# Two attention layers in one run each: queries and keys made a head ahead, projections 200 columns ahead, fewer small operations

## The chip, the cores and the metric

The kernel runs on one core of a Trainium2 chip. The metric is the device time of one execution in microseconds (us): 1171.78 us median of three runs (1171.17 to 1171.89). The engines are TensorE (PE, with its weight loads PEld), VectorE (DVE), ScalarE (ACT), GpSimd (POOL) and SyncE (SP), which issues most DMAs here. Each engine works off its own instructions in the order in which they stand.

## The reference

A decoder trunk of two layers on 512 tokens of 1024 features, all in float32. Each layer is attention and then a squared-ReLU MLP, both behind an RMS norm and with a residual.

```python
for layer in range(DEPTH):
    h = rms_norm(x, g_mix[layer])
    x = x + (even_mixer if layer % 2 == 0 else odd_mixer)(h, ...)
    h = rms_norm(x, g_mlp[layer])
    x = x + squared_relu_mlp(h, w_up[layer], w_down[layer])
```

Both mixers project h with one weight matrix, normalize q and k per head of 64 features (RMS, with a gain), attend and project the heads' outputs back. Layer 0 has eight heads of kind a (a mixture of dilated windows with a distance penalty) and eight of kind b (a window of 128, with two heads of k and v and a sink per head). Layer 1 has 16 heads of kind c (causal, with a bias c[t] - c[s] from a cumulated forget gate).

## The kernel before, in words

Every float32 matmul is three: the operands are split into a high part and the rest, and the products high x high, rest x high and high x rest are added up. For a weight tile the split is `parts` (a cast on ACT or POOL makes `whi`, a subtraction on DVE or POOL, L155, makes `wlo`).

In attention two streams of work are interleaved. The dense stream is `project` (L231 to L233): groups of 256 or 512 columns of q and k, or of v, over 32 pairs of feature chunk and token tile, and at the end of a layer `out_part`, the output projection. The results stand in four PSUM banks (`pA`); `norm_heads` copies them out (ACT), sums squares (ACT, then L250 on DVE), takes the reciprocal square root in small operations on DVE, and multiplies (L260), two token tiles on DVE and two on POOL. `prep_v` does the same for v without the norm.

The other stream is `attend`. It goes through pairs of heads. `get` makes a pair's q and k: `head_T` transposes (`qkT`, L267) into a bank of the other four (`pB`), and `prep_q` and `prep_k` write for each head a tile with the high part in one half of the partitions and the rest in the other (q), or both parts in both halves (k; the second half is copied by a DMA, L290). Each of the four query tiles i of a head is then scored (`S`, L325, L326), reduced with its bias on DVE (L339, which gives p and the negative maximum), exponentiated on ACT (L342, which gives the denominator), and scaled by the denominator's reciprocal (L345, then L350 on POOL or, for the last tile, L347 on ACT). In `values`, transposes (`PT`, L362) and products with v (`O`, L382) follow; a head's values are made within the scores of the next head.

`run` decides how the streams are woven. It takes a piece of the dense stream whenever that is behind its share, where `lead` shifts the share, and it is called once for each section: in layer 0 for a heads 0 to 3, for the b heads, and for the last a heads; in layer 1 once for each group of four heads. A section ends when its dense stream does; what is left of the attention is then run off. So a group's q and k are first asked for in the section after the one that projects them.

A scheduler then orders the instructions of each engine from this program order and from estimates of their durations, and gives out buffers as they come free.

Of the kernel before, what the change touches and what calls it, by code (L numbers as in the profile page):

```python
# [37 lines left out]
NORM = 'vgvg'  # L38
PSC = 'ggga'
GRAIN = 4  # L40
STARTPIN = 4
# [8 lines left out]
AHEAD = ()  # L50
# [13 lines left out]
LEADS = (0.0, 0.0, -0.16, 0.33, -0.3, -0.23, -0.09)  # L64
LAGS = (1, 1, 1)
NB = 86
# [6 lines left out]
def trunk(ctx, tc, x, g_mix, g_mlp, w_in_even, a_q_gain, a_k_gain, b_q_gain, b_k_gain, b_sinks,  # L73
# [118 lines left out]
    def layer_attention(li, hT, w_in, w_out, stats=None):  # L192


        with ExitStack() as c2:
# [44 lines left out]
            def norm_heads(outs, nh, sq_tag="sq", sq_bufs=1 + li):  # L240
# [11 lines left out]
                for t in range(NT):  # L252
                    nc.vector.tensor_scalar(v[:, t, :nh], ss[:, t, :nh], 1.0 / HD, ecol[:, t:t + 1],
                                            op0=OP.mult, op1=OP.add)
                rs = small.tile([P, NT, 8], F32, tag="rs", name="rs")
                rsqrt_small(rs[:, :, :nh], v[:, :, :nh])
                for t in range(NT):
                    q = qk[t // 2][:, t % 2, :w].rearrange("p (h d) -> p h d", d=HD)
                    eng = nc.gpsimd if NORM[t] == "g" else nc.vector
                    eng.tensor_mul(q, q, rs[:, t, :nh].unsqueeze(2).to_broadcast([P, nh, HD]))  # L260
# [9 lines left out]
            def prep_q(qk, off):  # L270

                pt = head_T(qk, off)
                q = ap.tile([P, 2, 512], F32R, tag="Q", bufs=2, name="Q")
                for h in range(2):
                    r = slice(h * HD, (h + 1) * HD)
                    r2 = slice((1 - h) * HD, (2 - h) * HD)
                    nc.scalar.copy(q[r, h], pt[r])
                    nc.vector.tensor_sub(q[r2, h], pt[r], q[r, h].bitcast(F32))
                return q

            def prep_k(qk, off, g):

                pt = head_T(qk, off)
                ks = []
                for h in range(2):
                    k = ap.tile([P, 2, 512], F32R, tag="K", bufs=3, name="K")
                    r = slice(h * HD, (h + 1) * HD)
                    r2 = slice((1 - h) * HD, (2 - h) * HD)
                    scale_split(k[r, 0], k[r, 1], pt[r], g[r])
                    nc.sync.dma_start(k[r2].bitcast(F32), k[r].bitcast(F32))  # L290
# [11 lines left out]
            def scores(q, k, j, kind, h, pr):  # L302
# [11 lines left out]
                rden = small.tile([P, NT], F32, tag="rden", name="rden")  # L314
                for i in range(NT):
# [29 lines left out]
                    nc.vector.reciprocal(rden[:, i:i + 1], den[:, i:i + 1])  # L345
                    if PSC[i] == "a":
                        nc.scalar.activation(p[:, :nv], p[:, :nv], AF.Copy, scale=rden[:, i:i + 1])  # L347
                    else:
                        eng = nc.gpsimd if PSC[i] == "g" else nc.vector
                        eng.tensor_scalar(p[:, :nv], p[:, :nv], rden[:, i:i + 1], 1.0, op0=OP.mult, op1=OP.mult)  # L350
# [52 lines left out]
            def attend(get, koff, V, vslot, kind, h0, np_, y0):  # L403

                for p_ in range(np_):
                    q, kk = get(p_)
# [23 lines left out]
            def run(att, n_att, dense, n_dense, lead=0.0):  # L430
# [12 lines left out]
                if att is not None:  # L443
                    for _ in att:
                        pass
# [798 lines left out]
```

## Time and profile before

| | |
|---|---|
| median of three runs | 1171.78 us |
| profiled execution | 1169.99 us, of which 1168.2 us span |
| PE busy | 1146.4 us (98%), 6256 matmuls |
| DVE busy | 879.8 us (75%), 1870 instructions |
| ACT busy | 646.6 us (55%) |
| POOL busy | 203.0 us (17%) |
| granted TensorE clock | 1.0 throughout |

Attention of layer 0 takes the time up to 228 us, its MLP the time to about 580 us, attention of layer 1 that to 831 us, and the second MLP the rest. In a busy row stand the time, the share of the span and the count of instructions. A group's row gives line, engine, operation, output and inputs with shapes, count, busy time, mean ns of one, and idle time of the engine just before with what ended it. A wait's row gives who waited for whom, total us, times, and the longest. Since matmuls are pipelined, a matmul's row is longer than the time to the next matmul's start.

### The profile page before, as it was taken

The page shows a single profiled execution, that of the slowest core. Times are in us where ns is not written, and L with a number is a line of the kernel's source. Part 1 is how long each engine was busy: PE and PEld are TensorE (multiplying, and loading weights), DVE is VectorE, ACT ScalarE, POOL GpSimd, SP SyncE. Part 2 cuts the span into 40 slices and gives each one's busy share as a digit, 9 for nine tenths or more (in the row PEclk, how much of TensorE's full clock was granted, in tenths as well). Part 3 has the DMA queues.
Part 4 walks back from the last instruction along what each step waited for, and adds up shares of the span by engine and source line. Part 5 has one row for each costly group of instructions (what it writes and reads, how often), then busy time and mean ns, then how long its engine had stood idle before and what let it go on. Part 6 is the DMA issues. An engine that isn't in the chain of part 4 may idle for free.

```text
span 1168.2 us, 17496 instructions
## 1 busy us (share of the span) xinstructions
PE 1146.4 (98%) x6256; PEld 981.4 (84%) x6256; DVE 879.8 (75%) x1870; ACT 646.6 (55%) x1349; POOL 203.0 (17%) x296
## 2 busy tenths in 40 slices
PE   8999989999999999999999999999999999999998
PEld 7987878887988988988887888888888888888887
DVE  7878999969947847855647877788858749669676
ACT  6556867655445545444335685656756455465452
POOL 1445434200000000000155445332100000000000
PEclk9999999999999999999999999999999999999999
DMA  7532024132332332333443323343430721623403
GB/s 257 160 91 73 19 73 145 58 123 73 101 117 91 91 108 91 96 121 108 148 127 109 103 89 110 100 124 112 163 106 3 232 91 51 202 73 108 148 34 109
DMA packets 100655, 126.57 MB, mean 108 GB/s; under 512 B 6184, under 2 KB 79944, under 8 KB 100568
## 3 DMA queue, kind: packets, MB, share of 16 engines
q1 hardware_dynamic: 99384, 121.23, 34.0%
q10 hardware_dynamic: 608, 2.13, 0.5%
q0 software_dynamic: 576, 2.10, 0.4%
q8 instruction: 49, 0.80, 0.3%
q14 instruction: 38, 0.31, 0.1%
HBM read 112.29 MB, written 6.32 MB: 102 GB/s over the span
## 4 chain that ended last, share of the span: by engine, by line
PE 82%; DVE 9%; DMA 3%; ACT 2%; POOL 1%; issue 1%; SPq 0%; ACTq 0%; POOLq 0%; DVEq 0%
PE up L164 10%; PE up L167 10%; PE up L168 10%; PE pj L231 4%; PE pj L233 4%; PE pj L232 4%; PE O L382 3%; PE PT L362 2%; PE Y L1023 2%; PE Y L1022 2%; PE Y L1020 2%; PE op L168 2%; PE op L164 2%; PE op L167 2%; PE S L325 2%; DVE wlo L155 1%
## 5 line engine op out<-in xcount | busy, mean ns | idle before, releaser
L164 PE MATMUL up<-xin,whi 128*128 128x512 f32 x512 | 200.5, 392 | 0.0
L168 PE MATMUL up<-xin,whi 128*128 128x512 f32 x512 | 199.3, 389 | 0.0
L167 PE MATMUL up<-xin,wlo 128*128 128x512 f32 x512 | 199.2, 389 | 0.0
L769 ACT CAST whi<-wraw 128x512 fp32r<-128x512 f32 x228 | 139.2, 619 | 105.5 <-PE up L168 47.3
L770 DVE TENSOR_TENSOR wlo<-wraw,whi 128x512 fp32r<-128x512 f32 x228 | 151.7, 686 | 53.7 <-ACT whi L769 53.5
L168 PEld LDWEIGHTS up<-xin,whi 128*128 128x128 f32 x512 | 96.1, 188 | 20.1
L164 PEld LDWEIGHTS up<-xin,whi 128*128 128x128 f32 x512 | 96.1, 188 | 19.9 <-issue 0.2
L167 PEld LDWEIGHTS up<-xin,wlo 128*128 128x128 f32 x512 | 96.2, 188 | 19.7 <-issue 0.2
L342 ACT ACTIVATE P<-P,negm 128x128 f32<-128x128 f32 (+5 forms) x128 | 69.6, 544 | 51.8 <-DVE negm L339 47.9
L231 PE MATMUL pj<-whi,hn 128*128 128x512 f32 (+2 forms) x256 | 88.7, 346 | 0.0
L951 ACT ACTIVATE u<-up 128x512 f32<-128x512 f32 x64 | 38.3, 598 | 90.9 <-PE up L168 90.9
L233 PE MATMUL pj<-whi,hn 128*128 128x512 f32 (+2 forms) x256 | 86.9, 339 | 0.0
L232 PE MATMUL pj<-wlo,hn 128*128 128x512 f32 (+2 forms) x256 | 86.8, 339 | 0.0
L152 POOL TENSOR_SCALAR whi<-wraw 128x512 fp32r<-128x512 f32 x88 | 61.1, 696 | 141.5 <-PE pj L233 121.3
L790 DVE TENSOR_TENSOR t<-u 128x256 f32<-128x256 f32 x56 | 23.2, 424 | 63.3 <-ACT u L1094 61.5
L155 POOL TENSOR_TENSOR wlo<-wraw,whi 128x512 fp32r<-128x512 f32 x48 | 64.4, 1345 | 20.8 <-ACT whi L150 18.1
L231 PE MATMUL pj<-whi,h 128*128 128x512 f32 (+1 forms) x192 | 65.6, 348 | 0.7 <-DVE v L160 0.7
L232 PE MATMUL pj<-wlo,h 128*128 128x512 f32 (+1 forms) x192 | 65.3, 341 | 0.2 <-DVE wlo L155 0.2
L233 PE MATMUL pj<-whi,h 128*128 128x512 f32 (+1 forms) x192 | 65.5, 343 | 0.0
L350 POOL TENSOR_SCALAR P<-P,rden 128x256 f32<-128x256 f32 (+2 forms) x96 | 47.7, 500 | 90.8 <-DVE rden L345 90.1
L155 DVE TENSOR_TENSOR wlo<-wraw,whi 128x512 fp32r<-128x512 f32 (+1 forms) x72 | 49.7, 697 | 17.5 <-POOL whi L152 9.8
L374 ACT CAST PT<-PT 128x256 fp32r<-128x256 f32 (+3 forms) x128 | 49.5, 405 | 19.3 <-PE PT L362 18.5
(229 smaller groups left out, 3051.7 us busy)
## 6 DMA issues: line engine op xcount, KB each, us to landing
wraw<-in_w_up SPq DMA_DIRECT2D x64, 512.0 KB, 4.0
wraw<-in_w_down SPq DMA_DIRECT2D x56, 512.0 KB, 4.2
wraw<-in_w_in_odd SPq DMA_DIRECT2D x36, 256.0 KB, 3.4
mraw<-in_w_down SPq DMA_DIRECT2D x16, 512.0 KB, 4.7
K<-K SPq DMA_DIRECT2D x26, 256.0 KB
wraw<-in_w_in_even SPq DMA_DIRECT2D x10, 512.0 KB, 4.0
wraw<-in_w_in_even SPq DMA_DIRECT2D x16, 256.0 KB, 4.5
xl<-xsp SPq DMA_DIRECT2D x8, 512.0 KB
```

Of the source, the lines that this page charges most:

```text
L152: nc.gpsimd.tensor_scalar(dst_h, src, 1.0, 1.0, op0=OP.mult, op1=OP.mult)
L155: in_order((nc.gpsimd if lo == "pool" else nc.vector).tensor_sub(dst_l, src, dst_h.bitcast(F32)))
L164: m = nc.tensor.matmul(o, wh, xh, start=start, stop=False, skip_group_check=more)
L167: nc.tensor.matmul(o, wl, xh, start=False, stop=False, skip_group_check=more)
L168: nc.tensor.matmul(o, wh, xl, start=False, stop=stop, skip_group_check=more)
L231: nc.tensor.matmul(o, xh, hi[:, :n], start=k == 0, stop=False)
L232: nc.tensor.matmul(o, xh, lo[:, :n], start=False, stop=False)
L233: nc.tensor.matmul(o, xl, hi[:, :n], start=False, stop=k == DC - 1)
L342: nc.scalar.activation(p[:, :ne], p[:, :ne], AF.Exp, scale=-1.0, bias=negm[:, i:i + 1], accum_out=den[:, i:i + 1])
L374: nc.scalar.copy(dst[:, 0], pt[:, :n])
L769: sca(nc.scalar.copy(dst_h, src))
L770: late.append(lambda: vec(nc.vector.tensor_sub(dst_l, src, dst_h.bitcast(F32))))
```

## The change: what it does

- `run` is called once for each layer. It gets a table of points (steps of attention, columns of the dense stream) and takes dense work whenever that is behind the line through the points. The points keep the dense stream 200 columns (`SKEW`) further than an even share.
- `attend` asks for the next pair's q and k right after the first score tile (`PRE` = 0) of a pair's second head, and `then` names the first pair of the next group, if that is projected by then. So `get` stands one head ahead, also from group to group.
- `prep_q` and `prep_k` cast and subtract once over all 128 partitions, that is for both heads, into a tile of the tag `acc`, whose four buffers also hold the residual sums; four DMAs of 64 partitions each then place q, and four place k.
- `norm_heads`: the scaling of the sums of squares is one operation and no longer four; all four multiplications are on DVE.
- `scores`: reciprocals of the first three tiles are taken at once, after the third tile's exponential, and the scalings follow.
- `ahead`, with an empty list before, is gone.

```diff
-                for t in range(NT):
-                    nc.vector.tensor_scalar(v[:, t, :nh], ss[:, t, :nh], 1.0 / HD, ecol[:, t:t + 1],
-                                            op0=OP.mult, op1=OP.add)
+                nc.vector.scalar_tensor_tensor(v[:, :, :nh], ss[:, :, :nh], 1.0 / HD,
+                                               ecol.unsqueeze(2).to_broadcast([P, NT, nh]), op0=OP.mult, op1=OP.add)
...
-                    eng = nc.gpsimd if NORM[t] == "g" else nc.vector
-                    eng.tensor_mul(q, q, rs[:, t, :nh].unsqueeze(2).to_broadcast([P, nh, HD]))
+                    nc.vector.tensor_mul(q, q, rs[:, t, :nh].unsqueeze(2).to_broadcast([P, nh, HD]))
...
             def prep_q(qk, off):
                 pt = head_T(qk, off)
+                both = act.tile([P, 2, 512], F32R, tag="acc", bufs=4, name="qs")
+                nc.scalar.copy(both[:, 0], pt)
+                nc.vector.tensor_sub(both[:, 1], pt, both[:, 0].bitcast(F32))
...
-                    nc.scalar.copy(q[r, h], pt[r])
-                    nc.vector.tensor_sub(q[r2, h], pt[r], q[r, h].bitcast(F32))
+                    nc.sync.dma_start(q[r, h].bitcast(F32), both[r, 0].bitcast(F32))
+                    nc.sync.dma_start(q[r2, h].bitcast(F32), both[r, 1].bitcast(F32))
...
             def prep_k(qk, off, g):
                 pt = head_T(qk, off)
+                both = act.tile([P, 2, 512], F32R, tag="acc", bufs=4, name="ks")
+                scale_split(both[:, 0], both[:, 1], pt, g)
...
-                    scale_split(k[r, 0], k[r, 1], pt[r], g[r])
-                    nc.sync.dma_start(k[r2].bitcast(F32), k[r].bitcast(F32))
+                    for r2 in (r, slice((1 - h) * HD, (2 - h) * HD)):
+                        nc.sync.dma_start(k[r2].bitcast(F32), both[r].bitcast(F32))
...
-                    nc.vector.reciprocal(rden[:, i:i + 1], den[:, i:i + 1])
...
+                    if i >= 2:
+                        i0 = 0 if i == 2 else 3
+                        nc.vector.reciprocal(rden[:, i0:i + 1], den[:, i0:i + 1])
...
-                    q, kk = get(p_)
+                    q, kk = pair.pop(0) if pair else get(p_)
...
+                            if j and i == PRE and p_ + 1 < np_:
+                                pair.append(get(p_ + 1))
+                            elif j and i == PRE and then is not None and then[0] in st:
+                                pair.append(then[1](0))
...
-            def run(att, n_att, dense, n_dense, lead=0.0):
+            def run(att, dense, points):
...
+                    (a0, d0), (a1, d1) = next((p, q) for p, q in zip(points, points[1:]) if a < q[0] or q is points[-1])
+                    if dense is not None and d < d0 + (d1 - d0) * (a - a0) / (a1 - a0):
...
-                run(att_a(0), 32, chain(kv_b(), project([(1536, 2048)], qk_use("b", 8))), 768, LEADS[0])
-                run(att_b(), NB, chain(qk_a(1), v_a(1)), 768, LEADS[1])
-                run(chain(att_a(1), last_values()), 38, chain(out_part([0, 1, 4, 5], True),
-                                                              out_part([6, 7], False), ahead([2, 3])), 1536, LEADS[2])
+                run(chain(att_a(0, (("qk", "b"), get_b)), att_b((("qk", 1), lambda p_: get_a(1, p_))), att_a(1), last_values()),
+                    chain(kv_b(), project([(1536, 2048)], qk_use("b", 8)), qk_a(1), v_a(1),
+                          out_part([0, 1, 4, 5], True), out_part([6, 7], False)),
+                    [(0, SKEW / 2), (33, 768 + SKEW), (109, 1536 + SKEW), (152, 2930)])
```

The built program shows where the work went. First TensorE before, in layer 1, at the pair whose scores use K_7699: the transposes qkT_7684 (q) and qkT_7694 (k) end the pair before, and projection matmuls (pj) follow them at once.

```order
L382 MATMUL O_7673<-PT3_6423,v1_6422 128x256
L267 MATMUL qkT_7684<-ident_72,qk_7082 128x128
L382 MATMUL O_7673<-PT3_6423,v1_6422 128x256 x3
L267 MATMUL qkT_7684<-ident_72,qk_7082 128x128
L267 MATMUL qkT_7684<-ident_72,qk_7083 128x128 x2
L267 MATMUL qkT_7694<-ident_72,qk_7082 128x128 x2
L267 MATMUL qkT_7694<-ident_72,qk_7083 128x128 x2
L233 MATMUL pj3_7563<-whi_7653,hn_6284 128x512
L231 MATMUL pj0_7560<-whi_7754,hn_6325 128x512
```

In all, 24 projection matmuls follow the transposes, and then comes the pair's first score, S_7725<-K_7699,Q_7689. After the change, the same engine and layer: the transposes qkT_7671 and qkT_7684 of a pair stand between the first two scores of the second head of the pair before it (K_7376).

```order
L326 MATMUL S_7664<-K_7376,Q_7360 128x256
L327 MATMUL S_7664<-K_7376,Q_7360 128x256
L329 LDWEIGHTS identb_77
L329 MATMUL S_7664<-maskb_87,identb_77 128x128
L263 MATMUL qkT_7671<-ident_72,qk_7115 128x128 x2
L263 MATMUL qkT_7671<-ident_72,qk_7116 128x128 x2
L263 MATMUL qkT_7684<-ident_72,qk_7115 128x128 x2
L263 MATMUL qkT_7684<-ident_72,qk_7116 128x128 x2
L326 MATMUL S_7698<-K_7376,Q_7360 128x256
L327 MATMUL S_7698<-K_7376,Q_7360 128x256
```

The pair's own first score follows only after that head's other scores, its values and six blocks of projection matmuls.

SP's queue before, at a pair of layer 1: the k tiles' second halves (K) between weights (wraw) and the bias of a head.

```order
L311 DMA bias_7467<-csp_93 128x512
L183 DMA wraw_8209<-in_w_in_odd 128x2x256 x2
L311 DMA bias_7546<-csp_93 128x512
L290 DMA K_7458<-K_7458 64x1024
L183 DMA wraw_8305<-in_w_in_odd 128x2x256
L290 DMA K_7462<-K_7462 64x1024
```

And after, where eight DMAs stand in a row for a pair, with the bias of a later head behind them:

```order
L311 DMA bias_7524<-csp_93 128x512
L181 DMA wraw_8019<-in_w_in_odd 128x2x256
L276 DMA Q_7360<-qs_7357 64x512 x2
L277 DMA Q_7360<-qs_7357 64x512 x2
L290 DMA K_7373<-ks_7370 64x1024 x2
L290 DMA K_7376<-ks_7370 64x1024 x2
L311 DMA bias_7659<-csp_93 128x512
```

At the start of layer 1's attention, TensorE after the change: the first transposes of all (qkT_6829, qkT_6842) stand 24 projection matmuls behind the end of the q and k projection that they need; before, 48.

```order
L231 MATMUL pj3_6793<-whi_6801,hn_6188 128x512
L263 MATMUL qkT_6829<-ident_72,qk_6750 128x128
L263 MATMUL qkT_6842<-ident_72,qk_6750 128x128
L229 MATMUL pj0_6790<-whi_6872,hn_6229 128x512
L230 MATMUL pj0_6790<-wlo_6873,hn_6229 128x512
L263 MATMUL qkT_6829<-ident_72,qk_6750 128x128
L263 MATMUL qkT_6842<-ident_72,qk_6750 128x128
```

They are spread among projection matmuls, one token tile at a time; before, all eight stood together.

More of the change, by code (lines that the diff above doesn't have):

```diff
@@ L37 @@
 WARM = 24
-NORM = 'vgvg'
 PSC = 'ggga'
 GRAIN = 4
+PRE = 0
 STARTPIN = 4
@@ L344, in scores @@
                     pr.append(p)
[L345 to L350, printed above, removed]
+                    ps_.append(p[:, :nv])
+                    if i >= 2:
+                        i0 = 0 if i == 2 else 3
+                        nc.vector.reciprocal(rden[:, i0:i + 1], den[:, i0:i + 1])
+                        for n in range(i0, i + 1):
+                            if PSC[n] == "a":
+                                nc.scalar.activation(ps_[n], ps_[n], AF.Copy, scale=rden[:, n:n + 1])
+                            else:
+                                nc.gpsimd.tensor_scalar(ps_[n], ps_[n], rden[:, n:n + 1], 1.0, op0=OP.mult, op1=OP.mult)
                     yield
@@ L401, in layer_attention, with attend @@
             last_head = [None]
-            def attend(get, koff, V, vslot, kind, h0, np_, y0):
+            pair = []
+            def attend(get, koff, V, vslot, kind, h0, np_, y0, then=None):
                 for p_ in range(np_):
-                    q, kk = get(p_)
+                    q, kk = pair.pop(0) if pair else get(p_)
                     yf = ap.tile([P, 512], F32, tag="yf", bufs=1, name="yf")
@@ L486, in layer_attention @@
             tiles = {}
-            def ahead(pairs):
-                for c0 in AHEAD:
-                    tiles[c0] = out_weights(pairs, c0)
-                    yield 0
             st = {}
@@ L581, in layer_attention @@
                 all_of(qk_c(0))
-                for g in range(3):
-                    run(att_c(g), 36, chain(qk_c(g + 1), v_c(g + 1)), 768, LEADS[3 + g])
-                run(chain(att_c(3), last_values()), 42, chain(out_part([0, 1, 2, 3], True),
-                                                              out_part([4, 5], False), ahead([6, 7])), 1536, LEADS[6])
+                run(chain(*[att_c(g) for g in range(4)], last_values()),
+                    chain(*[f(g) for g in range(1, 4) for f in (qk_c, v_c)],
+                          out_part([0, 1, 2, 3], True), out_part([4, 5], False)),
+                    [(0, SKEW / 2), (33, 768 + SKEW), (71, 1536 + SKEW), (109, 2304 + SKEW), (152, 3700)])
                 last = [6, 7]
```

55 lines of the change are left out of this document (27 added, 28 removed).

## The prediction

> **What bounds the kernel now.** I read the busy times of the page first, then the stretches of the two attention stages, then what TensorE (PE) waited for in them, and last the order of time around the longest waits.
>
> ```profile
> span 1168.2 us, 17496 instructions
> PE 1146.4 (98%) x6256; PEld 981.4 (84%) x6256; DVE 879.8 (75%) x1870; ACT 646.6 (55%) x1349; POOL 203.0 (17%) x296
> ```
>
> PE is the bound of the program: only 21.8 of 1168.2 us are without a matmul. The change leaves the number of matmuls as it is, so it can gain only what PE idles where attention runs. The next answer gives busy time by stretch (length; PE, PEld, DVE, ACT, POOL; clock; DMA share; GB/s). The first four stretches are layer 0 (heads 0 to 3 of kind a, the eight heads of kind b, the next three a heads, the output projection), the last two are layer 1.
>
> ```profile
> 54.00:108.00 54.00, 51.81 (x285) 43.39 (x284) 42.69 (x127) 30.50 (x80) 28.86 (x41) 1.00 0.31 93
> 108.00:172.00 64.00, 60.45 (x395) 52.47 (x394) 59.88 (x189) 48.05 (x140) 27.73 (x65) 1.00 0.12 38
> 172.00:199.00 27.00, 26.29 (x145) 21.52 (x144) 25.49 (x69) 19.30 (x50) 13.36 (x17) 1.00 0.56 166
> 199.00:228.00 29.00, 28.70 (x142) 23.64 (x141) 26.17 (x52) 17.19 (x36) 6.79 (x8) 1.00 0.24 74
> 600.00:627.00 27.00, 26.18 (x120) 21.41 (x118) 15.57 (x30) 8.07 (x13) 14.57 (x16) 1.00 0.38 115
> 627.00:822.00 195.00, 192.72 (x1194) 165.12 (x1195) 154.34 (x423) 124.41 (x303) 80.73 (x109) 1.00 0.38 109
> ```
>
> PE's idle time is 2.2 + 3.6 + 0.7 + 0.3 + 0.8 + 2.3 = 9.9 us, and that is about all there is to win. From 108 to 199 us DVE is busy 94% of the time: there it holds PE back. In layer 1 DVE is at 79%, and what PE waits for is something else:
>
> ```profile
> PE S L325 <- DVE Q L278: 1.8, 2, 1.5
> PE S L325 <- DVE yf L386: 1.8, 2, 1.6
> PE qkT L267 <- DVE qk L260: 1.3, 2, 0.9
> PE O L382 <- DVE PT L375: 0.6, 1, 0.6
> PE S L325 <- ACT v L159: 0.2, 1, 0.2
> ...
> PE S L325 <- DMA K<-K: 2.6, 3, 1.2
> PE O L382 <- DVE PT L375: 0.3, 1, 0.3
> ```
>
> The first five are layer 0, the last two layer 1 (total, times, longest). Most stand at a seam: the first score (S) of a pair of heads waits for the q and k that were made just before it. The idle time understates a wait, since a matmul is shown longer than the time to the next one:
>
> ```profile
> 625.56 0.39 PE L231 MATMUL pj<-whi,hn 128*128 128x512 f32 x1
> 625.79 0.39 PE L232 MATMUL pj<-wlo,hn 128*128 128x512 f32 x1
> 627.40 0.35 PE L325 MATMUL S<-K,Q 128*128 128x256 f32 x1 [1.23 <-DMA K<-K]
> 623.83 3.44 DMA K<-K
> ```
>
> Matmuls of 512 columns follow each other at 0.23 us; here 1.61 us passed, so 1.38 are lost where 1.23 are shown. I add 0.16 us a wait. Starts of matmuls that lie over 0.13 us too far apart are 28 in both stages, so the most that can be won is 9.9 + 28 x 0.16 = 14.4 us.
>
> **The change, part by part.** First the work, from these groups (busy us, mean ns | idle before):
>
> ```profile
> L278 DVE TENSOR_TENSOR Q<-qkT,Q 64x512 fp32r<-64x512 f32 x32 | 22.1, 689 | 3.9 <-ACT Q L277 3.0
> L345 DVE RECIPROCAL rden<-den 128x1 f32<-128x1 f32 x128 | 19.9, 158 | 7.2 <-ACT P L342 5.2
> L160 DVE SCALAR_TENSOR_TENSOR K<-qkT,gg,K 64x512 fp32r<-64x512 f32 x26 | 19.5, 749 | 0.7
> L260 DVE TENSOR_TENSOR qk<-qk,rs 128x512 f32<-128x512 f32 x14 | 17.1, 1262 | 0.2
> L253 DVE TENSOR_SCALAR ssv<-ss,ecol 128x8 f32<-128x8 f32 x28 | 9.6, 362 | 0.2
> L481 DVE TENSOR_TENSOR acc<-op,acc 128x512 f32<-128x512 f32 x32 | 21.7, 684 | 2.7 <-PE op L168 2.5
> L277 ACT CAST Q<-qkT 64x512 fp32r<-64x512 f32 x32 | 18.6, 582 | 28.6 <-PE qkT L267 20.4 <-DVE Q L278 7.9
> L260 POOL TENSOR_TENSOR qk<-qk,rs 128x512 f32<-128x512 f32 x14 | 18.9, 1367 | 15.1 <-DVE rs L134 14.6 <-issue 0.4
> ```
>
> - q for both heads in one subtraction: 32 become 16 on DVE, 16 x 0.689 = 11.0 us less; on ACT 16 x 0.582 = 9.3 us less. A tile of 128 partitions costs what one of 64 does (L481: 0.684 for 128x512).
> - k likewise: 13 x 0.749 = 9.7 us less on DVE, about as much on ACT.
> - reciprocals: 128 become 64, 10.1 us less; 32 small scalings (L253) become 8, 24 x 0.362 = 8.7 less. The reciprocals of the first three query tiles now wait for the third tile's exponential, and POOL's three scalings behind them come at once, 1.5 us together. Who waits is the transposes PT, which stand in the next head: at nothing.
> - the norm's multiplications all on DVE. Beside POOL's they took 1.262 us; alone I put them at L481's 0.69. 14 at 1.262 become 28 at 0.69: 19.3 for 17.7 us, and POOL loses its 18.9.
>
> DVE loses some 38 of the 324 us that the six stretches show. Off the bound this is worth nothing by itself. In the stretch 108 to 172 I count by the order what falls there: 4 Q subtractions, 16 reciprocals, 3 scalings and a K fewer (-7.1), four multiplications of 0.69 for two of 1.262 (+0.2), and two residual adds that now fall in it (+1.4): 59.9 to 54.4 us.
>
> Second, the order. A pair's transposes (qkT), casts and its eight DMAs now stand a head ahead, between the first two scores of the head before. In layer 1 a pair had some 24 projection matmuls (5.5 us) between its transposes and its first score; it now has a whole head, 12 to 15 us counted at 0.23 and 0.12 us a matmul. The chain that must fit is cast 0.58, subtraction 0.69, cast and subtraction of k 1.4, eight issues of some 0.45 us and a landing of 3.4: 10 us if nothing overlaps. So the K waits (2.6 + 3 x 0.16 = 3.1 us) go. The rows of SP:
>
> ```profile
> SPq L290 <- DVE K L160: 63.8, 24, 16.6
> ...
> 666.59 0.47 SPq L290 DMA_DIRECT2D K<-K  x1
> ```
>
> What is behind the DMAs on SP's queue is the bias of the next head and weights that are split a projection ahead; before, K's DMAs waited there 63.8 us for DVE in all, up to 16.6 at once, without a matmul missing its weights. The new tiles take two of the four buffers of the residual sums; the order puts the last pair's DMAs of layer 0 ahead of the third sum. I cost that at nothing; without that cover it is the fourth rival. [...]
>
> The norm chain of the b queries: its transposes now stand 16 us of matmuls behind the projection, before 4 to 9. That removes the qkT wait (1.3 + 2 x 0.16) and what followed it, 2.0 us in the stretch 54 to 108. The O wait there stays.
>
> In the stretch of the b heads I expect no gain. This is the seam at 150 us:
>
> ```profile
> 146.54 2.53 POOL L155 TENSOR_TENSOR wlo<-wraw,whi 128x512 fp32r<-128x512 f32 x2
> 146.84 1.01 DVE L253 TENSOR_SCALAR ssv<-ss,ecol 128x8 f32<-128x8 f32 x1
> 147.85 1.52 DVE L308 SCALAR_TENSOR_TENSOR bias<-dist,lb 128x256 f32<-128x256 f16 x1
> 149.37 0.41 DVE L308 SCALAR_TENSOR_TENSOR bias<-dist,lb 128x256 f32<-128x256 f16 x1
> 151.10 0.68 DVE L278 TENSOR_TENSOR Q<-qkT,Q 64x512 fp32r<-64x512 f32 x1
> 151.84 0.39 PE L325 MATMUL S<-K,Q 128*128 128x256 f32 x1 [1.52 <-DVE Q L278]
> ```
>
> While POOL subtracts, DVE stands: the same bias operation takes 1.52 and then 0.41 us. The late Q is DVE's backlog, and making Q earlier moves the backlog to the scores' reduction (L339), which frees the PSUM banks. And the new order leaves less there: between the first scores of b head 0 and of the next a head I count 49 us of matmuls where there were 57, the rest having moved ahead of it (a block of 47 projection matmuls stands between the b transposes and the first b score). DVE needs 54.4 at 94 to 96% use: 57 to 58 us, so PE loses 8 there, and it loses 64 - 57 = 7 now. I take 0 (between -3, if DVE fills every gap, and +6, if its 59.9 stay because POOL's subtractions stop it as often), nearer to the tally than to either end. The three a heads behind gain 0.3.
>
> Layer 1's start: the transposes stood 48 projection matmuls (10.9 us) behind the q and k projection, now 24 (5.5 us). What must come between:
>
> ```profile
> 609.19 0.59 ACT L247 COPY qk<-pj 128x512 f32<-128x512 f32 x1 [0.27 <-PE pj L233]
> 615.60 2.15 DVE L260 TENSOR_TENSOR qk<-qk,rs 128x512 f32<-128x512 f32 x2
> 615.72 2.93 POOL L260 TENSOR_TENSOR qk<-qk,rs 128x512 f32<-128x512 f32 x2 [3.12 <-DVE rs L134]
> 619.88 1.04 PE L267 MATMUL qkT<-ident,qk 128*128 128x128 f32 x8
> ```
>
> From 609.2 to 618.65 the chain takes 9.5 us; three scalings fewer take 0.8 off, and four multiplications of 0.69 end 0.2 us sooner. The first transposed tile is ready after 6 us, the last after 8.4, where PE comes by at 5.5 and 7.5: a new wait of about 0.8 us. Two heads in which the next norm chain falls have 12 us of matmuls beside some 13 us of DVE; I put 1.5 us on them. Against that go the K waits (3.1) and the O and PT waits of layer 1 (0.5 shown, six places with 0.16 each): -4.6 + 0.8 + 1.5 = -2.3.
>
> Sum: -2.0 + 0 - 0.3 - 2.3, and -0.4 for the first score of the program (its wait on ACT's v above, 0.2 + 0.16; it now has 8 instead of 5 us of matmuls behind its transposes): -5.0. The profiled execution took 1169.99 us (span 1168.2 and 1.8 around it), so 1165.0; the median of the runs shown, 1171.78, lies 1.8 higher: 1166.8 us.
>
> **The rivals.**
> - All attention waits go, since DVE, 38 us lighter, keeps up among the b heads too: 9.9 us idle and 1.5 of the hidden part, 1160.4. For it: DVE's 94% is the only thing that binds there. Against it: POOL's subtractions, which stop DVE, are as many as before.
> - The waits only move: 5 us taken at the seams come back at the transposes behind the norm chains and in the b heads (49 us of matmuls against 54.4 of DVE work). 1171.8. For it: DVE's use there, and the 5.5 us at layer 1's start.
> - Slower: DVE sets the b heads' time outright. If its work stays 59.9 us, that stretch takes 62 us for 49 of matmuls: 13 lost for 7, +6; the next stretch and longer norm waits +3.6; seams -4.6: 1176.8. It decides once DVE's work among the b heads is above 57 us (57 at 94% are 60.6, 11.6 lost for 7: the 4.6 of the seams). [...]
> - The DMAs come late: Q and K, issued one behind the other and each also waiting for DVE on SP's queue, hold up bias or weights. At 1 us for each of 16 pairs: 1177.8, after the gains above.
>
> **How the numbers follow.** The forecast has 0.50, all waits gone 0.18, waits only move 0.18, DVE the bound 0.10, DMAs late 0.04. A measurement of this kernel tells 0.2%, 2.3 us, from no change. Of the forecast a tenth falls within that (0.05); of the case where waits only move two thirds do (0.12), 0.02 end faster and 0.04 slower: faster 0.45 + 0.18 + 0.02 = 0.65, same 0.17, slower 0.04 + 0.10 + 0.04 = 0.18. The forecast's own range is 1162 to 1171. To hold 8 in 10 it must take in the full gain and part of the slower cases: 1160 to 1174.
>
> **What would show it.** Right: no K or Q wait before an S of layer 1; no qk wait at the b transposes; DVE's busy time some 25 to 35 us smaller; POOL's 20 smaller; PE's idle time among the b heads as large as before, under DVE. Wrong: a wait of PE on DVE among the b heads above 10 us, a wait of matmuls for weights, or a qkT wait at layer 1's start of several us.

## The result: 6.0 us slower, and the profile after

The changed kernel takes 1177.67 us (median of 4 runs, 1176.21 to 1178.75), the kernel before in the same session 1171.65 (4 runs). The ratio is 1.0051, with a 95% interval of 1.0034 to 1.0069. The forecast was 1166.8 us, and the range, up to 1174, does not hold the result.

The page of the changed kernel (its profiled execution took 1178.75 us, with a span of 1176.8) has these busy times:

```profile
span 1176.8 us, 17539 instructions
PE 1153.9 (98%) x6256; PEld 987.7 (84%) x6256; DVE 853.1 (72%) x1769; ACT 630.8 (54%) x1320; POOL 182.1 (15%) x280
```

DVE lost 26.7 us and POOL 20.9, within the signs that the forecast gave (25 to 35, and 20), and PE does the same 6256 matmuls. Four of the stretches shown before (length; PE, PEld, DVE, ACT, POOL; clock; DMA share; GB/s):

```profile
54.00:108.00 54.00, 51.27 (x275) 42.52 (x273) 39.70 (x114) 27.33 (x74) 26.27 (x36) 1.00 0.46 122
108.00:172.00 64.00, 61.82 (x394) 54.52 (x395) 51.35 (x158) 44.30 (x128) 23.27 (x59) 0.97 0.36 92
600.00:627.00 27.00, 24.70 (x105) 19.67 (x104) 13.69 (x26) 6.82 (x11) 10.97 (x12) 0.94 0.41 116
627.00:822.00 195.00, 191.67 (x1177) 162.87 (x1177) 135.92 (x363) 113.80 (x283) 73.05 (x104) 1.00 0.57 149
```

The work has moved within layer 0: the reductions of the b heads run from 123 to 174 us, before from 110 to 164, so the second row holds other work than the same row before. Two things strike the eye. PE idles more at layer 1's start (2.3 us of 27, 0.8 before) and behind it (3.3 us of 195, 2.3 before). And the granted clock, 1.00 throughout before, is 0.97 and 0.94 in two rows. What PE waited for, first in layer 0, then in layer 1 (total, times, longest):

```profile
PE O L386 <- DVE PT L379: 1.7, 3, 1.1
PE PT L366 <- DVE yf L390: 1.2, 1, 1.2
PE S L326 <- DVE yf L390: 1.1, 1, 1.1
PE PT L366 <- DVE rsq L131: 0.7, 1, 0.7
PE PT L366 <- POOL P L354: 0.6, 2, 0.4
...
PE qkT L263 <- DVE qk L256: 2.3, 2, 1.5
PE O L386 <- ACT PT L378: 2.0, 3, 1.4
PE S L326 <- DVE qs L271: 1.1, 1, 1.1
```

The waits that the forecast wanted gone are gone: no S waits for a DMA of K in layer 1 (2.6 us before), no qkT waits for qk in layer 0 (1.3). Others stand in their place. Three of them, in layer 1, and a change of the clock have to be followed to their source.

**Layer 1's start.** The transposes come by 24 projection matmuls behind the projection, and qk is not there. After the second wait matmuls of 512 columns start 0.43 us apart and no longer 0.23:

```profile
618.69 0.44 PE L263 MATMUL qkT<-ident,qk 128*128 128x128 f32 x2 [1.52 <-DVE qk L256]
620.37 0.44 PE L263 MATMUL qkT<-ident,qk 128*128 128x128 f32 x2 [0.78 <-DVE qk L256]
620.90 0.63 PE L229 MATMUL pj<-whi,hn 128*128 128x512 f32 x1
621.33 0.63 PE L263 MATMUL qkT<-ident,qk 128*128 128x128 f32 x2
```

**The clock.** Adjoining windows of 3.41 us, among the b heads and at layer 1's start:

```profile
149.80:153.22 3.42, 2.23 (x13) 1.53 (x12) 3.42 (x12) 2.16 (x9) 0.61 (x4) 1.00 0.00 0
153.22:156.63 3.41, 3.41 (x17) 3.19 (x17) 2.91 (x9) 2.67 (x8) 1.44 (x3) 0.50 0.00 0
...
617.43:620.84 3.41, 1.38 (x7) 0.94 (x8) 3.38 (x4) 0.00 (x0) 2.25 (x2) 1.00 0.48 154
620.84:624.25 3.41, 3.41 (x11) 2.60 (x10) 1.67 (x4) 1.59 (x3) 0.00 (x0) 0.50 0.02 5
624.25:627.66 3.41, 3.41 (x16) 2.78 (x15) 1.05 (x2) 0.86 (x1) 0.62 (x1) 1.00 0.85 185
```

Of the two windows before the half-clock ones PE was busy in 2.23 of 3.42 us and in 1.38 of 3.41. At half the clock for 3.41 us at most 1.7 us of work are lost, by my estimate; in the window from 620.84 us the matmuls' starts lie some 1.5 us further apart than their widths need. In this execution the clock fell to 0.50 four times: at these two places, and at 9.86 and 293.17 us, behind gaps of up to 1.87 us at the program's start and of 2.54 in the first MLP. In the profiled execution of before, with gaps of up to 1.93 and of 2.54 us at the same places of the program, it stayed at 1.00. The two executions stand further apart (8.8 us) than the medians do (6.0).

**The residual sums.** Q's and K's new tiles take two of the four buffers of the tag `acc`. DVE waits for the DMAs that read them. Behind the sum stands the reciprocal of a head's last tile, behind that its scaling on ACT, then ACT's copy of PT, and then the head's values on PE:

```profile
799.65 0.69 DVE L494 TENSOR_TENSOR acc<-op,xl 128x512 f32<-128x512 f32 x1 [2.47 <-DMA Q<-qs]
800.26 0.15 DVE L349 RECIPROCAL rden<-den 128x1 f32<-128x1 f32 x1
800.45 0.72 ACT L352 ACTIVATE P<-P,rden 128x512 f32<-128x512 f32 x1 [1.37 <-DVE rden L349]
801.48 0.38 PE L386 MATMUL O<-PT,v 128*128 128x256 f32 x1 [1.45 <-ACT PT L378]
```

**A weight that is late.** ACT stands until a weight has landed, the cast of q stands behind it, DVE's subtraction behind that, and the next score waits for that subtraction. It uses neither q nor k of the new pair, so what it can wait for is the PSUM bank of qkT:

```profile
767.34 0.38 SPq L181 DMA_DIRECT2D wraw<-in_w_out_odd  x1
772.09 0.62 ACT L148 CAST whi<-wraw 128x512 fp32r<-128x512 f32 x1 [1.78 <-DMA wraw<-in_w_out_odd]
772.74 0.59 ACT L270 CAST qs<-qkT 128x512 fp32r<-128x512 f32 x1
773.35 0.69 DVE L271 TENSOR_TENSOR qs<-qkT,qs 128x512 fp32r<-128x512 f32 x1 [1.51 <-ACT qs L270]
774.10 0.44 PE L326 MATMUL S<-K,Q 128*128 128x384 f32 x1 [1.08 <-DVE qs L271]
```

Why is the weight late? Q's and K's DMAs do not hold it up: SP issues nothing between 756.0 and 766.37 us. There a bias, which is ahead of the weight on SP's queue, stands until DVE has done the work that it waits for (issuer, who ended the wait, total us, times, longest):

```profile
SPq L311 <- DVE PT L379: 10.6, 1, 10.6
```

From its issue at 767.34 us the weight took another 4.7 us. Such a wait is not new: before the change ACT's longest for a weight, from 740 to 830 us, was 1.8 us too. New is that the cast of q stands behind it.

### The profile page after: what moved, and what is told of

Its sections match the earlier page's. It is cut to its first block, busy times and chain, and to the rows that moved or that the text cites. A ratio compares the mean times of both kernels' runs of the same rounds, so it can differ in the third digit from the quotient of the medians.

```text
span 1176.8 us, 17539 instructions
## 1 busy us (share of the span) xinstructions
PE 1153.9 (98%) x6256; PEld 987.7 (84%) x6256; DVE 853.1 (72%) x1769; ACT 630.8 (54%) x1320; POOL 182.1 (15%) x280
## 4 chain that ended last, share of the span: by engine, by line
PE 86%; DVE 6%; ACT 2%; POOL 2%; DMA 2%; issue 1%; SPq 0%; ACTq 0%; POOLq 0%; DVEq 0%
PE up L162 10%; PE up L165 10%; PE up L166 10%; PE pj L229 5%; PE pj L231 5%; PE pj L230 5%; PE O L386 2%; PE op L166 2%; PE op L165 2%; PE PT L366 2%; PE op L162 2%; PE Y L1035 2%; PE Y L1034 2%; PE Y L1032 2%; PE Y L1081 1%; PE Y L1084 1%
## 5 line engine op out<-in xcount | busy, mean ns | idle before, releaser
L340 DVE CUSTOM_DVE_ANT_0 P<-S,bias 128x128 f32<-128x128 f32 (+1 forms) x96 | 45.8, 483 | 19.0 <-PE S L329 11.5
```

## The experiments

Each kernel ran in turn with the kernel before on one chip. The chip's sessions differ a little, so what counts is the ratio to the kernel before of the same session; the changed kernel's is 1.0051. The interval of a ratio is 0.0009 to 0.0018 to each side, so two kernels are told apart from about 0.002 (2.3 us); smaller differences need a trace beside them. Differences below are those of the ratios. Line numbers shift by a few from kernel to kernel.

| kernel | edit | median us | ratio (95%) |
|---|---|---|---|
| e1_lead | 48 matmuls ahead of layer 1's first transposes | 1177.78 | 1.0056 (1.0043 to 1.0068) |
| e2_slots | last pair's q, k in own buffers | 1175.50 | 1.0037 (1.0024 to 1.0049) |
| e3_direct | q, k made as before | 1185.36 | 1.0120 (1.0105 to 1.0136) |
| e4_ops | before, with the small operations | 1173.58 | 1.0020 (1.0011 to 1.0029) |
| e5_norm | half of the norm on POOL | 1174.16 | 1.0021 (1.0009 to 1.0033) |
| e6_recip | a reciprocal for each tile | 1172.10 | 1.0005 (0.9996 to 1.0014) |
| e7_slots_opsold | e2, old small operations | 1175.87 | 1.0039 (1.0027 to 1.0052) |
| e8_late | q, k not a head ahead | 1207.12 | 1.0302 (1.0287 to 1.0318) |
| e9_slots_recip | e2 and e6 | 1171.57 | 1.0006 (0.9994 to 1.0018) |
| e10_slots_recip_lead | e1, e2 and e6 | 1171.67 | 0.9999 (0.9988 to 1.0009) |
| e11_pair | reciprocals for two tiles | 1175.73 | 1.0037 (1.0024 to 1.0050) |
| e12_brecip | before, reciprocals as changed | 1174.88 | 1.0028 (1.0017 to 1.0040) |
| e13_srl_patop | e10, a weight's cast off ACT | 1169.05 | 0.9975 (0.9965 to 0.9984) |
| e14_srl_patop_norm | e13 and e5 | 1170.96 | 0.9992 (0.9983 to 1.0002) |
| e15_after_patop | changed, that cast off ACT | 1175.05 | 1.0029 (1.0017 to 1.0042) |
| e16_before_patop | before, that cast off ACT | 1171.11 | 0.9997 (0.9988 to 1.0006) |
| e17_e13_batched | e13, reciprocals as changed | 1176.20 | 1.0035 (1.0022 to 1.0048) |
| e18_e13_skew100 | e13, SKEW 100 | 1177.40 | 1.0044 (1.0029 to 1.0058) |

### One part at a time

**e1_lead**, layer 1's transposes later:

```diff
-                    [(0, SKEW / 2), (33, 768 + SKEW), (71, 1536 + SKEW), (109, 2304 + SKEW), (152, 3700)])
+                    [(0, 200), (33, 768 + SKEW), (71, 1536 + SKEW), (109, 2304 + SKEW), (152, 3700)])
```

> The changed kernel with layer 1's table of points starting at (0, 200) instead of (0, 100): 48 instead of 24 projection matmuls stand between the end of the q and k projection and the first transposes. Theory A (the time was lost at single places: TensorE waits at layer 1's start, at the residual sums and at late weights, and each longer gap is followed by a stretch at half the granted clock): the qkT waits at layer 1's start (1.68 + 0.95 us between starts) go, and with them the half-clock stretch that followed them (about 1.5 us); 2.5 to 4 us less than the changed kernel's 1177.7, so 1174 to 1175. Theory B (the 64 + 52 DMAs that place q and k, and the 15 MB more that they move, delay weights everywhere): nothing at the start is theirs, 1177 to 1178. Theory C (the norm chain, now on DVE alone, makes everything behind it late): the wait shrinks but comes back at the first scores, 1176 to 1178.

Both qkT waits and the half-clock window are gone from layer 1's start (mean granted clock of the profiled execution 0.997, of the changed kernel's 0.994), and the time is the same. Around 655 us, in the head in which the next norm falls, O waited for PT (0.9 and 0.9 us between starts too much) and a projection for v (1.1). Theory A fails here: the wait had moved, as theory C has it, and the time lies in C's range, though the new waits are not at the first scores.

**e2_slots**, the last pair's tiles elsewhere:

```diff
-                both = act.tile([P, 2, 512], F32R, tag="acc", bufs=4, name="qs")
+                both = slot("qs") if spare else act.tile([P, 2, 512], F32R, tag="acc", bufs=4, name="qs")
```

(the same for `ks`; `spare` is the last pair of layer 1, and `slot` gives a tile of the tag `act`.)

> The changed kernel with the q and k of layer 1's last pair of heads written to two tiles of the tag act (free by then, the projections being over) and no longer to two of the four acc buffers. Theory A: the third residual sum need not wait for the DMAs that read those tiles; DVE's 2.5 us of waiting for Q<-qs and the 1.6 us gap of TensorE between the output projection and the values of that head go: 1.3 to 1.7 us less than the changed kernel, about 1176. Theories B and C: the DMAs are as many and DVE as busy; within 0.5 us of 1177.7.

The wait of DVE for Q<-qs and the gap of PE at 800 us are gone from the trace. The time falls by 1.6 us by the ratios, as expected for that gap. The intervals overlap, so it is the trace that shows the effect and not the time.

**e3_direct** has `prep_q` and `prep_k` of the kernel before, all else as changed.

> The changed kernel's order and small operations, but q and k made as before the change: cast and subtracted for each head alone, K's second half by one DMA of a tile, Q without a DMA. Theory A: the residual sums' wait (1.6) and the late weights' wait near the last heads (1.3) go, DVE and ACT get some 20 us of work back, of which the b heads lose 2 to 4: 1175 to 1179. Theory B: nearly all of the loss goes, 1171 to 1173, and weights land after 3.6 us (median) and not 4.5. Theory C: no faster, 1178 to 1181.

8 us slower than the changed kernel, and above what any of the three theories allowed: theory B falls. The placing by DMA is a gain in this order. It halves what DVE spends on q and k (22.1 + 19.5 us before, 11.0 + 9.7 changed), and ACT's part too. Without it PE stood 2.7 us in the stretch of 199 to 232 us, with DVE busy 91% of it; the changed kernel had no idle time of PE from 199 to 228 us. That DVE's load is the whole of the 8 us is not shown.

**e8_late** never asks ahead:

```diff
-                            if j and i == PRE and p_ + 1 < np_:
+                            if False:
...
-                            elif j and i == PRE and then is not None and then[0] in st:
+                            elif False:
```

> The changed kernel with each pair's q and k asked for at the pair's own first score and no longer a head ahead; all else as changed. The first scores then wait for the whole chain of cast, subtraction and eight DMAs, some 10 us of which the order covers part: 16 pairs at 2 to 5 us, 1200 to 1250, with waits of S on the DMAs of Q and K. If the scheduler moves other work in between (rival), under 1190.

29 us slower than the changed kernel, within the range expected, so the placing by DMA pays only with the head of lead. The longest wait is the first score's for K, as expected, but all such waits come to 8.3 us; the output projection of layer 0 waits 6.1 us too, for PSUM banks that DVE empties late (first layer 0, then layer 1):

```profile
PE op L162 <- DVE acc L494: 6.1, 4, 2.3
PE S L326 <- DMA K<-ks: 4.5, 1, 4.5
...
PE S L326 <- DMA K<-ks: 3.8, 3, 1.7
```

### The small operations

**e4_ops** is the kernel before with the diff's lines on `ssv`, the norm and the reciprocals.

> The kernel before with the small operations alone changed: one scaling of the sums of squares, reciprocals of three tiles at once, all four multiplications of the norm on DVE; order and q and k as before. Theory A: DVE is some 18 us lighter but off the bound; 1169.5 to 1171.5 against the kernel before's 1171.7. Theory B: the same. Theory C: slower than before by 2 us or more, with longer qk and rs waits behind POOL's subtractions.

2.3 us slower: theory C, that the small operations harm, is the one that holds. Its place for the loss does not: the waits of qkT for qk are as long as before (1.3 us), and the longest new one is O's for PT, 2.5 us at 764 us, with a half-clock window behind it (mean granted clock of the execution 0.995). **e5_norm** and **e6_recip** take one of them back in the changed kernel:

```diff
-                    nc.vector.tensor_mul(q, q, rs[:, t, :nh].unsqueeze(2).to_broadcast([P, nh, HD]))
+                    (nc.gpsimd if t % 2 else nc.vector).tensor_mul(q, q, rs[:, t, :nh].unsqueeze(2).to_broadcast([P, nh, HD]))
```

```diff
-                    if i >= 2:
-                        i0 = 0 if i == 2 else 3
-                        nc.vector.reciprocal(rden[:, i0:i + 1], den[:, i0:i + 1])
...
+                    nc.vector.reciprocal(rden[:, i:i + 1], den[:, i:i + 1])
```

e5_norm:

> The changed kernel with two of the norm's four multiplications back on POOL. In the kernel before with only the small operations changed, the four stand in a row on DVE (2.5 us) ahead of a PT subtraction that TensorE waited 2.6 us for; in the changed kernel they take 3.6 us at layer 1's start, beside POOL's subtraction. Theory C1 (this row of four is the loss): the wait at layer 1's start falls by 1 to 1.5 us, waits of O for PT go, 2 to 3 us faster than the changed kernel: about 1175. Rival C2 (POOL's and DVE's multiplications shut each other out anyway, two at 1.26 us each are as long as four at 0.62): within 1 us of 1177.7.

3.5 us less than the changed kernel, as theory C1 wants, but only in part where it said: the waits of O in layer 1 are gone, while at layer 1's start PE still loses 2.8 us between starts, in three pieces. e6_recip:

> The changed kernel with a reciprocal for each query tile and its scaling at once, as before. Theory C3 (taking three reciprocals together delays the scalings on POOL, and so the transposes PT and what follows): PT no longer waits for POOL's P, the waits of O for PT shrink, 1 to 3 us faster than the changed kernel, 1175 to 1177, although DVE has 10 us more to do. Rival C2 (the reciprocals stand in nobody's way, and DVE is the fuller for it): 1178 to 1180.

5.4 us less, with 64 more instructions on DVE: more than theory C3 allowed. In e6_recip DVE is busy 852.4 us, in the changed kernel 853.1: of the 9.4 us that the fewer reciprocals save, nothing is left in DVE's sum. (The norm's multiplications alone took 23.1 us in the changed kernel and 21.2 in e6.) Some of the 5.4 us stand at places that other edits mend too: in e6's trace the gap of 1.62 us at the residual sums is gone, and that of the score behind q's subtraction is 0.66 us, not 1.33. So the gains of the single edits do not add up. **e7_slots_opsold** takes back all small operations and has e2's buffers:

> The changed order and the placing of q and k by DMA, with the tiles of the last pair in their own buffers, but all small operations as before the change. The small operations alone cost the kernel before 2.2 us; the buffers gave 2.2 back. If the two parts add up: 1173 to 1174. If the small operations are needed with the new order (DVE lighter among the b heads): 1176 to 1178.

It is 3.9 us above e9 (below), which differs from it in the norm's multiplications and in the scaling of the sums of squares. So what half of the norm on POOL is worth depends on the rest: it gained 3.5 us in the changed kernel, lost 2.0 in e14, at the edge of what can be told apart, and lost 3.9 here together with the old scaling. No rule on the norm follows from these runs.

**e11_pair** (`if i % 2: i0 = i - 1`) and **e12_brecip** (the kernel before with this edit alone):

e11_pair:

> The changed kernel with the reciprocals taken for two tiles at a time (0 and 1, 2 and 3) in place of three and one: DVE has as few of them as in the changed kernel, but a tile waits for one later exponential and no longer for two. Theory F (the delay of the first tiles' scaling is what costs): about half of the 5.6 us come back, 1174 to 1176. Rival G (the scheduler's other order is what helped, not the delay): no telling, 1172 to 1179, with waits at other places than those of the run with one reciprocal for each tile.

e12_brecip:

> The kernel before with only the reciprocals taken as in the change, three and then one. Theory F: the delay costs there too, 2 to 4 us, 1173.5 to 1175.5, with waits of PT for POOL's P or of O for PT. Rival G: within 1 us of the kernel before, 1171 to 1172.5, since DVE is off the bound in most stretches.

By the ratios the reciprocals of three tiles cost 3.3 us in the kernel before and 5.4 in the changed one, and those of two tiles lie between (1.6 less than three, 3.7 more than one). That looks like theory F, but the waits are not the ones that it names: PT waited for POOL's P 0.2 us in e12, 0.6 in the changed kernel. e12's longest gap, 3.07 us before a score at 196 us, is the chain of the late weight again, this time over POOL and DVE:

```profile
190.15 1.21 POOL L152 TENSOR_SCALAR whi<-wraw 128x512 fp32r<-128x512 f32 x2 [4.01 <-DMA wraw<-in_w_out_even]
190.81 1.09 DVE L155 TENSOR_TENSOR wlo<-wraw,whi 128x512 fp32r<-128x512 f32 x1 [3.08 <-POOL whi L152]
191.93 0.69 DVE L278 TENSOR_TENSOR Q<-qkT,Q 64x512 fp32r<-64x512 f32 x1
```

The scheduler had put the weight's subtraction ahead of q's. How much of the price is the delay of the scalings and how much the order that follows from it stays open.

### Together

**e9_slots_recip** has the edits of e2 and e6:

> The changed kernel with both edits that gave time back: the last pair's q and k in their own buffers, and a reciprocal for each query tile. If the two causes are apart (theory D): 5.6 + 2.2 us less than the changed kernel, about 1170. If the reciprocals' edit already ended the wait at the residual sums, since DVE's order is another (rival; in that run DVE waits 0.6 + 0.5 us for Q<-qs in place of 2.5): 1171.5 to 1172.5.

**e10_slots_recip_lead** has that of e1 besides:

> The same with layer 1's table starting at (0, 200), so that 48 projection matmuls stand ahead of its first transposes. Theory D: the qkT waits at layer 1's start (1.68 + 0.94 us) go and do not come back, since the waits of O for PT that took their place in the first such run came from the late reciprocals: 2 to 3 us less than the kernel without this edit, 1167 to 1169. Rival E (whatever is taken away at the start comes back in the next two heads, where DVE is full): no less than without it.

e9 is level with e6 (the rival: the other order of DVE had shortened the wait for Q already), and e10 level with e9, as rival E has it. e10's trace shows why: the qkT waits are gone, the O waits that replaced them in e1 are smaller, and 2.66 us more between starts, with a half-clock window behind (mean granted clock of the execution 0.996), stand in one place:

```profile
766.62 0.62 ACT L148 CAST whi<-wraw 128x512 fp32r<-128x512 f32 x1 [3.13 <-DMA wraw<-in_w_out_odd]
767.27 0.58 ACT L270 CAST qs<-qkT 128x512 fp32r<-128x512 f32 x1
768.63 0.69 PE L325 MATMUL S<-K,Q 128*128 128x384 f32 x1 [2.41 <-DVE qs L271]
```

Of PAT_OP, which says who casts and who subtracts a weight tile of the output projection, one entry was therefore changed, in e10 (**e13**), there with e5's norm (**e14**), in the changed kernel (**e15**) and in the kernel before (**e16**):

```diff
-PAT_OP = (('pool', 'pool'), ('pool', 'dve'), ('pool', 'dve'), ('act', 'pool'))
+PAT_OP = (('pool', 'pool'), ('pool', 'dve'), ('pool', 'dve'), ('pool', 'pool'))
```

e13_srl_patop:

> The kernel with the three edits (last pair's own buffers, a reciprocal for each tile, 48 matmuls ahead of layer 1's first transposes), and the fourth weight tile of each block of the output projection cast on POOL and no longer on ACT. Theory H (ACT, waiting 3.1 us for a weight's DMA with the cast of q behind it, is what takes back the gain at layer 1's start): the S wait on qs (2.4 us) and the half-clock stretch behind it (about 1.5) go, 3 to 4 us less than 1171.7: 1167.5 to 1169. Rival I (POOL then waits, with the scaling of P behind it, or DVE takes the wait over): 1171 to 1173.

e14_srl_patop_norm:

> The same, with two of the norm's four multiplications on POOL. The four on DVE take 2.9 us in a row among the b heads, with a wait of S for yf of 1.6 us and a half-clock stretch behind it. If that row is the loss: 2 to 3 us less than the kernel without this edit. If the two engines shut each other out (a run with all old small operations stood at 1175.9): no gain, or up to 4 us more.

e15_after_patop:

> The changed kernel with only this cast moved from ACT to POOL. Its trace shows the same chain at 773 us, with a wait of 1.1 us (1.33 between starts) and 1.6 more at the residual sums, which this edit leaves. Theory H: 1 to 1.5 us less than 1177.7, 1176 to 1177. Rival I: 1177 to 1179.

e16_before_patop:

> The kernel before with only this cast moved. There ACT waits 2.7 us for weights in two places, but q and k are made earlier or later than these: its trace shows no TensorE wait from it. Theory H and rival I: within 1 us of the kernel before, 1171 to 1173; below 1170.5, the edit would be a gain by itself and say nothing on the change.

Theory H holds: e13 is 2.8 us below e10, a little less than the 3 to 4 expected, and 2.9 below the kernel before, whose ratio of 1 lies outside its interval. So it beats both kernels. In the kernel before the same edit does nothing, as expected. In the changed one it gives 2.6 us where 1 to 1.5 were expected, and its interval overlaps with that of the changed kernel. e14 is 2.0 us above e13: half of the norm on POOL gains nothing here. Layer 1's attention in e13, in two stretches, and all of its waits there:

```profile
600.00:627.00 27.00, 27.00 (x125) 22.45 (x124) 14.72 (x27) 6.17 (x12) 13.38 (x15) 1.00 0.45 122
627.00:822.00 195.00, 193.17 (x1189) 163.87 (x1189) 142.63 (x407) 115.36 (x287) 76.20 (x107) 1.00 0.56 149
...
PE O L382 <- DVE PT L375: 0.5, 1, 0.5
PE S L325 <- issue: 0.3, 1, 0.3
PE O L382 <- ACT PT L374: 0.2, 1, 0.2
PE S L325 <- DVE qs L271: 0.2, 1, 0.2
```

Last, e13 with the reciprocals of the change (**e17**) and with `SKEW = 100` (**e18**). e17_e13_batched:

> The fastest kernel so far (1169.05) with the reciprocals taken for three tiles at once and then for one, as in the change; all else as there. Theory F (the delay of the first tiles' scaling costs in any order): 3 to 5.6 us more, 1172 to 1174.7. Rival G (it was the scheduler's order in single cases): within 1.5 us, 1168 to 1170.5.

e18_e13_skew100:

> The fastest kernel so far with the projections 100 columns ahead of an even share in place of 200. Theory J (the lead is what gives a pair's norm chain its time, and half of it leaves the chain short): waits of qkT for qk of 0.5 to 1 us at three or four groups, 1171 to 1173. Rival K (a head of matmuls stands between anyway): within 1 us, 1168 to 1170.

e17: 7.0 us more, above what theory F allowed, and this is the run that shows the delay at work. Between starts, five of them stand from 640 to 760 us and two from 120 to 200. The waits in layer 1 are those of O for PT, which ACT and DVE copy late in the head of a norm, with a half-clock window behind at 656 us (mean granted clock of the execution 0.997):

```profile
PE O L386 <- DVE PT L379: 1.7, 3, 0.7
PE O L386 <- ACT PT L378: 1.0, 2, 0.7
PE pj L229 <- DVE v L158: 0.5, 1, 0.5
PE PT L366 <- POOL P L354: 0.2, 1, 0.2
```

In e17 the three scalings of that head start together at 653.4 us, some 4.4 us behind the head's last score; in e13 they start at 646.0, 648.4 and 651.1, that score at 647.0. e18: 8.1 us more, above both expectations. One qkT wait of 1.4 us is theory J's; the longest wait, 3.1 us with a half-clock window behind it at 792 us (mean granted clock of the execution 0.994), is the weight's chain over POOL and DVE once more.

## Why the prediction was wrong

What each matmul's start lies further from the one before than its width needs (0.227 us for 512 columns, 0.173 for 384, 0.119 for 256, 0.109 for 128), summed by stretch, worked out from the three traces (the bounds are fixed times, so work near a bound can change sides):

| us | 20-60 | 60-120 | 120-200 | 200-280 | 600-640 | 640-760 | 760-820 |
|---|---|---|---|---|---|---|---|
| before | 1.9 | 4.7 | 8.6 | 1.3 | 2.0 | 5.6 | 1.8 |
| changed | 0.7 | 5.5 | 10.2 | 0.9 | 4.9 | 5.4 | 5.1 |
| e13 | 0.7 | 4.5 | 7.2 | 0.6 | 1.4 | 6.0 | 2.1 |

Layer 0 (20 to 280 us) lost 17.3 us after 16.5, where the forecast had 2.7 less; layer 1 lost 15.4 after 9.4, where it had 2.3 less. Most of the error is in layer 1. Every sign that the forecast named for being right came true, since they belong to what it had priced. Of the signs for being wrong one came in part, the qkT wait at layer 1's start. What failed were mainly terms put at nothing.

- **The small operations, at nothing: the step that failed most.** "Who waits is the transposes PT, which stand in the next head: at nothing." PT does wait little for the scalings (0.6 us), but the reciprocals' edit cost 5.4 us in this kernel (e6), 3.3 in the kernel before (e12) and 7.0 in e13 (e17). In e17 the delay is seen in the head of a norm: the scalings start late, and O waits for PT 2.7 us in layer 1. The working did not look past PT to O, and it took the order of the rest as given, which the scheduler changes when an operation of each head comes later. How much of the price is the one and how much the other stays open.
- **Layer 1's start, +0.8: mis-sized.** The waits are 1.68 + 0.95 us between starts, and the half-clock window behind them costs some 1.5 more. The working let the norm's chain run undisturbed; in the trace a weight's subtraction on DVE stands within it, and the four multiplications, beside a subtraction on POOL, took 3.58 us, not 2.8. Over the program 28 of them took 0.89 us each, not 0.69:

```profile
617.94 3.58 DVE L256 TENSOR_TENSOR qk<-qk,rs 128x512 f32<-128x512 f32 x4
617.95 1.81 POOL L153 TENSOR_TENSOR wlo<-wraw,whi 128x512 fp32r<-128x512 f32 x1
L256 DVE TENSOR_TENSOR qk<-qk,rs 128x512 f32<-128x512 f32 x28 | 23.1, 887 | 0.2
```

- **The clock was not priced at all.** Each long gap was costed at its own length; the half-clock window behind the waits at layer 1's start added some 1.5 us.
- **The buffers of the sums, at nothing: failed.** The order was looked at for layer 0, where the DMAs do come first; in layer 1 the third sum came to wait (1.6 us).
- **Layer 1's waits, -4.6: gone for K, but not as time.** K's waits (3.1 of the 4.6) are gone: Q's pieces of 128 KB landed after 2.9 us and K's of 256 KB after 4.7 (medians), and no score of layer 1 waited for them. But O waits for PT at two other places, 660 and 715 us (0.39 and 0.54 between starts), and from 640 to 760 us PE loses 5.4 us after 5.6. The late weight's 1.33 us and the sums' 1.62 stand in the last column (760 to 820, +3.3).
- **The b heads, 0: right, and for the reason given.** From the first reduction of a b head to that of the next a head, before and after:

```profile
109.60:172.80 63.20, 59.81 (x391) 52.23 (x392) 59.27 (x189) 47.32 (x138) 27.15 (x63) 1.00 0.14 42
123.10:180.00 56.90, 54.53 (x363) 48.24 (x362) 52.45 (x167) 42.26 (x129) 24.36 (x60) 0.97 0.35 89
```

The forecast had 57 to 58 us with 54.4 of DVE's work; it took 56.9 with 52.45, below the 57 at which the rival of DVE as the bound was to decide. Summed as in the table, PE lost about 7.9 us there and 7.6 before.

- **The b queries, -2.0: the wait went, the gain did not come.** In place of the qkT waits O waits for PT (1.23, 0.44 and 0.49 between starts), and 60 to 120 us lost 5.5 us after 4.7. The program's start gained 1.2 (20 to 60 us): the first score's 0.4, as forecast, and a projection's wait for v at 48 us (0.87), which the forecast did not count.

Of the rivals, the one of the late DMAs gave 1177.8 us, 0.1 from the result, and that is luck. Its sum takes some 10 us of gains off where the forecast has 5.0, and with 5.0 it would give 1182.8. Its cause has a part of the truth at one place and not at sixteen pairs: the sums wait for Q's DMAs. The late weight (2.6 us by e15) stood behind a bias that waited for DVE, not behind Q or K. That the change could gain was right: with four things mended (the reciprocals, the sums' buffers, layer 1's start and the weight's cast), e13 is 2.9 us faster than before, where the forecast was 5.0. By the table its gain stands in layer 0 (13.0 us after 16.5); layer 1 lost 9.5 us after 9.4, so the 2.3 forecast there did not come even so.

## What to carry to other kernels

An operation that is batched to save its engine's time is also later, and in a kernel that a scheduler orders the price need not be found where it was changed: measure each such edit alone before adding it to a large change. When a transfer or a buffer is moved, follow each engine past the instruction that waits: a weight's DMA, for which ACT waited 1.78 us, became a wait of 1.08 us for a score on PE, and the DMA itself was late because of what stood ahead of it on its queue (a bias, for 10.6 us). And a gap of PE can cost more than its own length: at layer 1's start the waits took 1.68 + 0.95 us between starts, and the window at half the clock behind them some 1.5 more.

## What the hardware showed that was not expected

The clock. In 17 of the 20 profiled executions the mean granted clock was 0.990 to 0.997, in the other three 0.999 to 1.000. In the changed kernel's trace it is 0.50 in four windows of 3.41 us while the program runs, and these lie on one grid through the whole execution: from 9.86 us to 153.22, 293.17 and 620.84 it is 42, 83 and 179 times 3.413 us. For each window of this grid, and of the grid in the trace of the kernel before, I summed the time that its matmuls need from start to start. In the four windows ahead of the half-clock ones this was 0.28 to 0.39 of the window; in the others, up to the last matmuls of the two traces, at least 0.43 (in the kernel before, from 7.23 us). The same gap, 2.54 us in the first MLP, has a half-clock window behind it in the one trace and none in the other: in the changed kernel 2.44 us of it lie in one window (0.28), while in the kernel before the grid divides it into 1.57 and 0.97 us (0.53 in the lower of the two windows). At layer 1's start two waits of 1.52 and 0.78 us in one window had the half clock behind them.

Small operations beside POOL. In the norm's chain an operation on 32 columns takes 0.18 us, and at one place, where POOL subtracts a weight beside it, 1.12 us (e17):

```profile
647.82 1.29 POOL L153 TENSOR_TENSOR wlo<-wraw,whi 128x512 fp32r<-128x512 f32 x1
648.04 1.12 DVE L132 SCALAR_TENSOR_TENSOR rsq<-rsq 128x32 f32<-128x32 f32 x1
650.13 0.18 DVE L132 SCALAR_TENSOR_TENSOR rs<-rsq 128x32 f32<-128x32 f32 x1
```
